# Holding back the first pair's two output stores in a single-core Winograd convolution

## The chip, the cores and the metric

The kernel runs on one core of a Trainium2 chip. The metric is the device time of one execution in microseconds (us), given as the median of several runs. A core has a matrix engine (TensorE, PE in the profile), three engines for elementwise work (VectorE or DVE, ScalarE or ACT, GpSimd or POOL), SyncE (SP), which here only issues transfers, and 16 DMA engines, which move everything between device memory and the on-chip memory.

## The reference

The kernel computes a 3x3 convolution with padding 1 over 16 images of 64 channels and 64x64 points, with 128 output channels, all float32:

```python
batch, c_in, h, w, c_out = 16, 64, 64, 64, 128
x_pad = np.pad(x, ((0, 0), (0, 0), (1, 1), (1, 1)), mode='constant')
...
output[b, co] += weight[co, ci, kh, kw] * x_pad[b, ci, kh:kh+h, kw:kw+w]
```

The input is 16.8 MB and the output 33.6 MB, so two thirds of the traffic are stores.

## The kernel before

**Pairs and blocks.** The images are taken two at a time: a pair's two images of 64 channels fill the 128 partitions. There are 8 pairs (`p`), and each is worked through in 4 blocks (`blk`) of 16 output rows. In a block, TensorE makes three groups of products per image, `U`, `A` and `Bt` (L154), each into a PSUM tile (tag `acc`; 8 such buffers). The row direction uses a short Winograd scheme: `U` comes from sums of neighbouring input rows (`ss`, made on GpSimd at L73 one pair ahead), and even and odd output rows are `A + U` and `Bt + U`. ScalarE copies `U` out of PSUM (`ut`, L168), and VectorE adds (L177 for even rows, L180 for odd rows) into the output tile `ot`.

**Output tiles.** Every image has its own `ot` tile of 128 x 4096 float32 (2 MB). They come in turn from `opool`, which has 7 buffers. The first two of these are lent to the float32 inputs of pairs 0 and 1 (`x0`, `x1`). So the buffers run: `x0`, `x1`, pair 0 (third and fourth), pair 1 (fifth and sixth), pair 2 (seventh and first), pair 3 (second and third), pair 4 (fourth and fifth), and so on. The first image of pair 0 and the second image of pair 3 share a buffer: the second L177 instruction of pair 3 may only write when the store of pair 0's first image has landed. Likewise pair 4's first image waits for the store of pair 0's second image.

**Transfers and their queues.** SP issues the loads of the weights and of `x0` and `x1` (L44 to L48). GpSimd issues the other six input loads (L59, pairs 2 to 7) one behind the other at the start; these read 2 MB of float32 each and write 1 MB of float16. The stores (L112) have two queues. For pairs 0 to 5 an image is stored whole, after its last block: the first image by SP (`store(nc.sync, ...)`, L182), the second by ScalarE. ScalarE's store is put into the list `held` (L184) and issued in the next block behind the two `ut` copies (L170, L171), so that ScalarE need not wait for VectorE. Pairs 6 and 7 are stored in halves of 1 MB. `keep` fixes the order of the instructions of an engine as it is written.

**Semaphores.** The transfers of SP and ScalarE take turns on a set of eight completion semaphores. A store that takes one up again first waits until the transfer that had it eight issues earlier has landed.

Of the kernel before, what the change touches and what calls it, by code (L numbers as in the profile page):

```python
# [12 lines left out]
@with_exitstack  # L13
def kernel(
    ctx: ExitStack,
    tc: tile.TileContext,
    x: bass.AP,
    weight: bass.AP,
    out: bass.AP,
):  # L20
    nc = tc.nc
    B, CI, H, W = x.shape
    CO = weight.shape[0]
    assert H == 64 and W == 64 and CI == 64 and CO == 128 and B % 2 == 0
    NP = B // 2
    RB = 8

    keep = tc.keep_in_program_order
    x_rows = x.rearrange("b c h w -> (b c) h w")
    out_rows = out.rearrange("b co h w -> b co h w")  # L30
    w_flat = weight.rearrange("co ci kh kw -> co (ci kh kw)")

    const = ctx.enter_context(tc.tile_pool(name="const", bufs=1))
    psum = ctx.enter_context(tc.tile_pool(name="psum", bufs=8, space=bass.MemoryType.PSUM))
    xpool = ctx.enter_context(tc.tile_pool(name="xpool", bufs=8))
    opool = ctx.enter_context(tc.tile_pool(name="opool", bufs=7))
    spool = ctx.enter_context(tc.tile_pool(name="spool", bufs=3))
    upool = ctx.enter_context(tc.tile_pool(name="upool", bufs=4))


    first = const.tile([48, 16], F32)
    nc.scalar.dma_start(first, x_rows[5 * 128 :: 8, 0, 0:16])
    w_raw = const.tile([CO, CI * 9], F32)
    nc.sync.dma_start(w_raw, w_flat)  # L44
    x0 = opool.tile([128, H, W], F32, tag="ot", name="x0")
    nc.sync.dma_start(x0, x_rows[0:128, :, :])
    x1 = opool.tile([128, H, W], F32, tag="ot", name="x1")
    nc.sync.dma_start(x1, x_rows[128:256, :, :])  # L48
    cuts = [(0, 18), (18, 34), (34, 50), (50, 64)]
    ident = const.tile([128, 128], F16)  # L50
    make_identity(nc, ident)
    w16 = const.tile([CO, CI * 9], F16)
    keep(nc.gpsimd.tensor_copy(w16, w_raw))  # L53

    xs = {0: xpool.tile([128, H, W], F16, tag="xs", name="xs")}

    def load(p):
        xs[p] = xpool.tile([128, H, W], F16, tag="xs", name="xs")
        keep(nc.gpsimd.dma_start(xs[p], x_rows[128 * p : 128 * p + 128, :, :]))  # L59

    xs[1] = xpool.tile([128, H, W], F16, tag="xs", name="xs")
    for p in range(2, NP):
        load(p)


    ss = {}

    def sums(eng, p, src, lo, n):
        if p not in ss:
            ss[p] = spool.tile([128, H // 2, W], F16, tag="ss", name="ss")  # L70
        v = src.rearrange("p (j i) c -> p j i c", i=2)
        keep(
            eng.tensor_add(  # L73
                ss[p][:, lo : lo + n, :], v[:, lo : lo + n, 0, :], v[:, lo : lo + n, 1, :]
            )
        )


    Wt = const.tile([128, 5, 3, CO], F16)
    G0, G21, G1, G01, G2 = range(5)  # L80

    def wrow(i):
        return Wt[:, i, :, :].rearrange("p t c -> p (t c)")

    wps = {}
    for kh in (1, 2, 0):
        wp = psum.tile([128, 512], F32, tag="acc", name="wp")
        for k in range(3):
            t = 3 * kh + k
            for q in (0, 64):  # L90
                nc.tensor.matmul(wp[q : q + 64, k * CO : k * CO + CO], w16[:, t::9], ident)  # L91
        wps[kh] = wp[:, 0 : 3 * CO]
    keep(nc.scalar.copy(wrow(G1), wps[1]))  # L93
    sums(nc.vector, 0, x0, 0, RB)
    keep(nc.vector.tensor_sub(wrow(G21), wps[2], wrow(G1)))  # L95
    keep(nc.vector.tensor_sub(wrow(G01), wps[0], wrow(G1)))  # L96
    for n, (lo, hi) in enumerate(cuts):
        keep(nc.scalar.copy(xs[0][:, lo:hi, :], x0[:, lo:hi, :]))  # L98
        if n == 0:
            keep(nc.scalar.copy(wrow(G0), wps[0]))  # L100
            keep(nc.scalar.copy(wrow(G2), wps[2]))  # L101
        if n < 3:
            sums(nc.vector, 0, x0, RB * (n + 1), RB)

    held = []

    whole = {3: (0, 64)}
    halves = {1: (0, 32), 3: (32, 64)}
    cuts_of = [(whole, whole)] * (NP - 2) + [(halves, halves)] * 2

    def store(eng, p, b2, ot, lo, hi):
        return eng.dma_start(  # L112
            out_rows[2 * p + b2, :, lo:hi, :],
            ot.rearrange("p j i c -> p (j i) c")[:, lo:hi, :],
        )

    for p in range(NP):
        if p + 1 < NP:
            for lo in (0, 16):
                sums(nc.gpsimd, p + 1, x1 if p == 0 else xs[p + 1], lo, 16)  # L120
        ots = [
            opool.tile([128, H // 2, 2, W], F32, tag="ot", name="ot") for _ in range(2)
        ]
        for blk in range(4):
            j0 = blk * RB

            def group(wi_rows):

                tiles = [
                    psum.tile([128, RB, W], F32, tag="acc", name="acc") for _ in range(2)  # L130
                ]
                n = 3 * len(wi_rows)
                i = 0
                for wi, off in wi_rows:
                    for kw in (1, 0, 2):
                        c_lo, c_hi = max(0, 1 - kw), min(W, W + 1 - kw)
                        for b2 in range(2):
                            p0 = 64 * b2
                            lo, hi = j0, j0 + RB
                            if off is None:  # L140
                                rhs = ss[p][p0 : p0 + 64, lo:hi, c_lo + kw - 1 : c_hi + kw - 1]
                            else:
                                while 2 * lo + off < 0:
                                    lo += 1
                                while 2 * (hi - 1) + off > H - 1:
                                    hi -= 1
                                first = 2 * lo + off
                                last = 2 * (hi - 1) + off
                                rhs = xs[p][
                                    p0 : p0 + 64,  # L150
                                    first : last + 1 : 2,
                                    c_lo + kw - 1 : c_hi + kw - 1,
                                ]
                            nc.tensor.matmul(  # L154
                                tiles[b2][:, lo - j0 : hi - j0, c_lo:c_hi],
                                Wt[p0 : p0 + 64, wi, kw, :],
                                rhs,
                                start=i == 0,
                                stop=i == n - 1,
                            )  # L160
                        i += 1
                return tiles

            U = group([(G1, None)])
            us = []
            for b2 in range(2):
                ut = upool.tile([128, RB, W], F32, tag="ut", name="ut")
                keep(nc.scalar.copy(ut, U[b2]))  # L168
                us.append(ut)
            while held:  # L170
                keep(store(nc.scalar, *held.pop(0)))  # L171
            if p == 0 and blk >= 2:
                for lo in (32 * blk - 64, 32 * blk - 48):
                    keep(nc.scalar.copy(xs[1][:, lo : lo + 16, :], x1[:, lo : lo + 16, :]))  # L174
            A = group([(G21, 1), (G0, -1)])
            for b2 in range(2):
                nc.vector.tensor_add(ots[b2][:, j0 : j0 + RB, 0, :], A[b2], us[b2])  # L177
            Bt = group([(G01, 0), (G2, 2)])
            for b2 in range(2):
                nc.vector.tensor_add(ots[b2][:, j0 : j0 + RB, 1, :], Bt[b2], us[b2])  # L180
            if blk in cuts_of[p][0]:
                store(nc.sync, p, 0, ots[0], *cuts_of[p][0][blk])  # L182
            if blk in cuts_of[p][1]:
                held.append((p, 1, ots[1], *cuts_of[p][1][blk]))  # L184
    while held:
        keep(store(nc.scalar, *held.pop(0)))
# [30 lines left out]
```

## Time and profile before

| what | value |
|---|---|
| time, median of 3 runs | 127.02 us (126.86 to 127.49) |
| profiled execution, its own time | 127.1 us |
| profiled execution, span of the instructions | 125.3 us |
| TensorE busy | 105.8 us (84%) |
| VectorE busy | 83.5 us (67%) |
| ScalarE busy | 44.5 us (36%) |
| GpSimd busy | 34.5 us (28%) |
| device memory read, written | 17.08 MB, 33.55 MB |
| a whole-image store, median from issue to landing | 20.3 us (SP), 20.1 us (ScalarE) |
| one input load of pairs 2 to 7, median from issue to landing | 29.7 us |

The profile was taken on one execution of 127.1 us, of which 125.3 us lie between its first and last instruction; the other 1.8 us lie outside. It is 0.1 us above the median of the runs. Times inside the profile count from the start of the span. DMA figures are given as the busy share of the 16 engines and as GB/s; the GB/s count the bytes written, so that a load which turns float32 into float16 shows half of what it reads.

### The profile page before, as it was taken

Reading aid. Unit: us, or ns where it says so; the run is one execution under the profiler, and the core shown is the slowest. Engines: PE = TensorE matmul, PEld = TensorE weight load, DVE = VectorE, ACT = ScalarE, POOL = GpSimd, SP = SyncE. Lnnn points to the kernel's source line nnn. Section 1 sums busy time; section 2 is a strip of 40 time slices with the busy share of each in tenths; the row PEclk is TensorE's granted clock in tenths of the full one; section 3 lists DMA queues with packets and bytes.
Section 4 is the critical chain, followed back from the end, with each engine's and each line's share of the span. In section 5 each row is a group of like instructions: output and inputs, shape, how many; then the busy total and the mean of one; then the engine's idle time right before and its main releaser. Section 6 shows DMA issues by size and latency. Waiting matters only on the chain.

```text
span 125.3 us, 2411 instructions
## 1 busy us (share of the span) xinstructions
PE 105.8 (84%) x978; PEld 53.8 (43%) x978; DVE 83.5 (67%) x134; ACT 44.5 (36%) x76; POOL 34.5 (28%) x27
## 2 busy tenths in 40 slices
PE   0407999999999999999999999999999999996000
PEld 0303454555455454555555455454545455452000
DVE  0009298787778777777787778788788878868000
ACT  4108938943333333333333333333333333331000
POOL 2750008999366005700480049000000000000000
PEclk9999999999999999999999999999999999999965
DMA  4999999999999999999999999999999999999980
GB/s 121 424 379 332 316 267 225 212 209 204 377 340 387 356 332 358 356 379 340 340 377 356 405 434 424 429 439 439 413 429 429 424 416 416 431 424 418 431 371 39
DMA packets 4250, 44.48 MB, mean 355 GB/s; under 512 B 528, under 2 KB 528, under 8 KB 656
## 3 DMA queue, kind: packets, MB, share of 16 engines
q1 hardware_dynamic: 1872, 21.27, 40.8%
q10 hardware_dynamic: 1504, 16.78, 31.6%
q0 software_dynamic: 864, 6.29, 24.6%
q8 instruction: 7, 0.11, 0.3%
q14 instruction: 3, 0.02, 0.0%
HBM read 17.08 MB, written 33.55 MB: 404 GB/s over the span
## 4 chain that ended last, share of the span: by engine, by line
PE 82%; DMA 7%; DVE 2%; issue 1%; DVEq 0%; SPq 0%
PE acc L154 82%; DMA x<-in_x_dram 7%; DVE ot L177 1%; DVE ss L73 1%; DVE ot L180 0%; DVEq L212 0%; SPq L44 0%; DVEq L177 0%
## 5 line engine op out<-in xcount | busy, mean ns | idle before, releaser
L154 PE MATMUL acc<-xs,Wt 64*128 64x504 f16 (+3 forms) x768 | 88.6, 377 | 0.0
L154 PEld LDWEIGHTS <-Wt 64*128 64x128 f16 x960 | 52.7, 95 | 55.8 <-issue 6.1
L177 DVE TENSOR_TENSOR ot<-acc,ut 128x512 f32<-128x512 f32 x64 | 41.2, 686 | 23.1 <-PE acc L154 18.4
L168 ACT COPY ut<-acc 128x512 f32<-128x512 f32 x64 | 34.4, 589 | 60.6 <-issue 38.5
L180 DVE TENSOR_TENSOR ot<-acc,ut 128x512 f32<-128x512 f32 x64 | 41.1, 684 | 0.0
L73 POOL TENSOR_TENSOR ss<-xs 128x1024 f16<-128x1024 f16 x12 | 25.2, 2122 | 28.9 <-PE acc L154 25.8
L154 PE MATMUL acc<-ss,Wt 64*128 64x504 f16 (+1 forms) x192 | 27.0, 384 | 4.3 <-DVE ss L73 4.3
L73 DVE TENSOR_TENSOR ss<-x 128x512 f16<-128x512 f32 x4 | 2.6, 685 | 9.5 <-DMA x<-in_x_dram 9.5
L73 POOL TENSOR_TENSOR ss<-x 128x1024 f16<-128x1024 f32 x2 | 4.7, 2358 | 11.5 <-DMA x<-in_x_dram 11.5
L98 ACT CAST xs<-x 128x1024 f16<-128x1024 f32 (+2 forms) x4 | 4.0, 1054 | 3.7 <-DMA x<-in_x_dram 3.7
L91 PE MATMUL wp<-ident,w 128*64 128x128 f16 x18 | 1.3, 327 | 4.6 <-POOL w L53 4.6
L174 ACT CAST xs<-x 128x1024 f16<-128x1024 f32 x4 | 4.0, 1058 | 0.0
L59 POOL DMA_DIRECT2D xs<-in_x_dram x6 | 3.4, 582 | 0.0
L91 PEld LDWEIGHTS <-w 128*64 128x64 f16 x18 | 1.1, 209 | 4.6 <-POOL w L53 4.6
L93 ACT ACT_TABLE_LOAD x1 | 1.3, 1283 | 1.2 <-PEq L201 1.2
L93 ACT CAST Wt<-wp 128x384 f16<-128x384 f32 x1 | 0.5, 479 | 2.8 <-PE wp L91 2.8
L53 POOL CAST w<-w_raw 128x576 f16<-128x576 f32 x1 | 0.7, 664 | 2.6 <-DMA w_raw<-in_weight_dram 2.6
L100 ACT CAST Wt<-wp 128x384 f16<-128x384 f32 x1 | 0.5, 478 | 0.5 <-DVE Wt L96 0.5
L95 DVE TENSOR_TENSOR Wt<-wp,Wt 128x384 f16<-128x384 f32 x1 | 0.6, 550 | 0.0
L96 DVE TENSOR_TENSOR Wt<-wp,Wt 128x384 f16<-128x384 f32 x1 | 0.5, 547 | 0.0
L101 ACT CAST Wt<-wp 128x384 f16<-128x384 f32 x1 | 0.5, 485 | 0.0
masks.py:199 POOL TENSOR_SCALAR_AFFINE_SELECT ident<-ident 128x128 f16<-128x128 f16 x1 | 0.3, 293 | 0.1
(5 smaller groups left out, 0.6 us busy)
## 6 DMA issues: line engine op xcount, KB each, us to landing
out_dram<-ot SPq DMA_DIRECT2D x6, 2048.0 KB, 20.3
out_dram<-ot ACTq DMA_DIRECT2D x6, 2048.0 KB, 20.1
xs<-in_x_dram POOLq DMA_DIRECT2D x6, 1024.0 KB, 29.7
x<-in_x_dram SPq DMA_DIRECT2D x2, 2048.0 KB, 13.0
out_dram<-ot SPq DMA_DIRECT2D x4, 1024.0 KB, 10.9
out_dram<-ot ACTq DMA_DIRECT2D x4, 1024.0 KB, 10.9
w_raw<-in_weight_dram SPq DMA_DIRECT2D x1, 288.0 KB, 3.1
first<-in_x_dram ACTq DMA_DIRECT2D x1, 3.0 KB, 2.9
```

The costliest lines, as they stand in the source:

```text
L53: keep(nc.gpsimd.tensor_copy(w16, w_raw))
L59: keep(nc.gpsimd.dma_start(xs[p], x_rows[128 * p : 128 * p + 128, :, :]))
L73: eng.tensor_add(ss[p][:, lo : lo + n, :], v[:, lo : lo + n, 0, :], v[:, lo : lo + n, 1, :])
L91: nc.tensor.matmul(wp[q : q + 64, k * CO : k * CO + CO], w16[:, t::9], ident)
L93: keep(nc.scalar.copy(wrow(G1), wps[1]))
L95: keep(nc.vector.tensor_sub(wrow(G21), wps[2], wrow(G1)))
L98: keep(nc.scalar.copy(xs[0][:, lo:hi, :], x0[:, lo:hi, :]))
L154: nc.tensor.matmul(tiles[b2][:, lo - j0 : hi - j0, c_lo:c_hi], Wt[p0 : p0 + 64, wi, kw, :], rhs, start=i == 0, stop=i == n - 1,)
L168: keep(nc.scalar.copy(ut, U[b2]))
L174: keep(nc.scalar.copy(xs[1][:, lo : lo + 16, :], x1[:, lo : lo + 16, :]))
L177: nc.vector.tensor_add(ots[b2][:, j0 : j0 + RB, 0, :], A[b2], us[b2])
L180: nc.vector.tensor_add(ots[b2][:, j0 : j0 + RB, 1, :], Bt[b2], us[b2])
```

## The change

The two stores of pair 0 are issued later, and both by ScalarE. Before, SP issued the store of pair 0's first image as soon as VectorE had finished it, and ScalarE issued the second image's store in the first block of pair 1. Now both are put into `held`, and `held` is not emptied until block 3 of pair 1, where ScalarE issues both behind its two `ut` copies. From there on everything is issued in the places where it was, so that pair 1's stores follow a block later.

```diff
-            while held:
+            while held and (p, blk) >= (1, 3):
                 keep(store(nc.scalar, *held.pop(0)))
...
-            if blk in cuts_of[p][0]:
+            if p == 0 and blk == 3:
+                held.append((p, 0, ots[0], 0, 64))
+            elif blk in cuts_of[p][0]:
                 store(nc.sync, p, 0, ots[0], *cuts_of[p][0][blk])
```

## The prediction

> **What bounds the kernel now.** I read first the page's slices of the span and its DMA queues, then the chain of work that ended last, then the busy time of chosen stretches, then landing times of single transfers, and last the timelines of VectorE and TensorE around the place where the moved store's buffer is needed again.
>
> The page's slices (40 of 3.13 us each; busy tenths, then GB/s written) and queues (packets, MB, share of the 16 engines):
>
> ```profile
> DMA  4999999999999999999999999999999999999980
> GB/s 121 424 379 332 316 267 225 212 209 204 377 340 387 356 332 358 356 379 340 340 377 356 405 434 424 429 439 439 413 429 429 424 416 416 431 424 418 431 371 39
> ...
> q1 hardware_dynamic: 1872, 21.27, 40.8%
> q10 hardware_dynamic: 1504, 16.78, 31.6%
> q0 software_dynamic: 864, 6.29, 24.6%
> ```
>
> The DMA engines are full from the second slice to the 38th; the three queues (SP, ScalarE, GpSimd) add up to 97% of 16 engines' span. The chain of waits, however, is nearly all TensorE:
>
> ```profile
> 10.21 103.29 PE acc L154 x948
> ```
>
> TensorE runs without a break from 10.2 to 113.5 us. Two limits therefore lie side by side, and the chosen stretches (length, then engines' busy time, clock, DMA share, GB/s written) show how close:
>
> ```profile
> 18.50:25.50 7.00, 7.00 (x68) 3.54 (x66) 5.71 (x10) 5.87 (x8) 6.15 (x3) 1.00 1.04 218
> 27.50:30.00 2.50, 2.50 (x28) 1.22 (x24) 2.01 (x4) 1.07 (x2) 2.50 (x2) 1.00 1.06 157
> 31.00:71.00 40.00, 40.00 (x379) 20.30 (x376) 31.66 (x51) 13.31 (x25) 13.97 (x7) 1.00 1.01 359
> 72.00:116.00 44.00, 42.68 (x402) 21.48 (x396) 34.95 (x56) 13.96 (x26) 4.20 (x2) 1.00 1.01 426
> 116.00:121.00 5.00, 0.00 (x0) 0.00 (x0) 0.04 (x1) 0.00 (x0) 0.00 (x0) 0.88 1.00 423
> 121.00:124.50 3.50, 0.00 (x0) 0.00 (x0) 0.00 (x0) 0.00 (x0) 0.00 (x0) 0.50 0.32 133
> ```
>
> Loads alone (18.5 to 25.5) write 218 GB/s, which is 436 read. Stores alone (72 to 116) move 426. Loads beside stores (31 to 71) write 359; GpSimd's last three loads fall there, and about 2.9 MB of what is written is theirs, so 73 GB/s more are read: 432. A byte costs the same in all three mixtures.
>
> The last stores are issued at 115.5 and 116.1 us and land at 124.2 and 124.4 us. From 116 on, 5.0 x 423 + 3.5 x 133 = 2.58 MB are still written; 2.10 MB of it are the two last stores themselves. Older backlog is thus only 0.48 MB, or 1.1 us. So the end moves with the DMA total, or with TensorE once TensorE is over 1.1 us later.
>
> **Part 1: the stores' bytes.** Nothing is added or removed: 20 stores before and after, the same sizes. Time is lost only if the DMA engines run empty, so I ask what they have to do between 25.8 us, where the stores were issued, and their new place. GpSimd's loads landed at 18.7, 24.1, 29.0, 42.5, 57.3 and 71.8 us (issue plus landing time of each). Without stores beside them, two follow each other by 4.9 us (24.1 to 29.0); with both store queues full, by 13.5 to 14.8 us. Without the stores, the last three would land at 33.9, 38.8 and 43.7 us. ScalarE issues the held stores behind the copies of pair 1's block 3: those start at 35.40, and at 25.75 the same pair of copies had its store 0.68 us later, so at 36.1, and the second 0.34 us later (one issue lasts 338 to 367 ns). The loads last till 43.7, so the engines stay full. Cost: 0. Loads that come earlier than before help nobody, since TensorE never waits for one after 10.2 us.
>
> **Part 2: the issuing engines.** SP loses one issue (0.33 us) that nothing waited for. Its store of pair 1's first image keeps its own place at 38.6. ScalarE loses one issue at 26.4 and has two at 36.1, 0.7 us in all. Behind them on ScalarE are the copies at 38.56, before which it sat idle for 2.09 us, so 1.4 us of cover remain. Without it, the 0.34 us more would be late into a PSUM buffer. Cost: 0. The semaphores go round in the same order as before, and the uses that come eight issues later wait for pair 0's stores at 77 us, long after any landing considered here.
>
> **Part 3: the wait for the buffer.** This is what the change can lose. Pair 3's second image takes the buffer of pair 0's first. Its need, on VectorE:
>
> ```profile
> 52.71 1.29 DVE L177 TENSOR_TENSOR ot<-acc,ut 128x512 f32<-128x512 f32 x2 [0.69 <-PE acc L154]
> ```
>
> The second of these two adds starts at 53.3 us. Before, the store had landed at 25.8 + 20.5 = 46.3, which left 7.0 us. Now it is issued 10.3 us later.
>
> ```profile
> L112 SPq DMA_DIRECT2D out_dram<-ot x1: 348/348/348, 25.8 to 25.8; - x1
> ...
> DMA to landing us min/median/max: 20.5/20.5/20.5
> ```
>
> With the same 20.5 us it would land at 56.6. With the longest landing of any whole-image store (22.9 us, issued at 51.4) it would land at 59.0; with the shortest (13.9 us, issued at 89.9, with two queues full) at 50.0. Between these I work it out. A 2 MB store costs the engines 2.10 / 426 = 4.9 us. The page's slices show that stores did not get going before about 30.1 us (204 GB/s up to 31 is still the loads' own rate), 4.3 us behind the issue. So the first held store starts at 40.4, when 43.7 - 40.4 = 3.3 us of loads remain. SP's store of pair 1 starts at 38.6 + 4.3 = 42.9. Until then two queues share: 1.25 us of work each. Then three share: the loads' 2.05 us take until 49.1, and the store has 1.6 us left, which at half the engines end at 52.3. The first store of the trace landed 1.5 us after the same reckoning (30.1 + 3 x 4.9 = 44.8 against 46.3), so I add 1.5: it lands at 53.8, half a microsecond late. I take this rather than a row of before, since before three loads stood against the store, and now two thirds of one.
>
> What does half a microsecond cost? TensorE's timeline:
>
> ```profile
> 51.12 2.69 PE L154 MATMUL acc<-xs,Wt 64*128 64x512 f16 x24
> ...
> 54.28 2.77 PE L154 MATMUL acc<-xs,Wt 64*128 64x512 f16 x24
> ```
>
> (The shapes that each row names are those of its first matmul.) A block takes six of the eight PSUM buffers. What the late add frees is next taken by the following block's `Bt`, the second half of the stretch that starts at 54.28, so at 55.6. The add ends at 54.0 in time, so it may be 1.6 us late before TensorE stops: landings up to 54.9 cost nothing there, and VectorE, idle about 0.7 us in each block, catches up. With the 1.1 us at the end, the end itself stays where it is for landings up to 56.0. Cost at 53.8: 0.
>
> Pair 0's second store follows on ScalarE's queue at half the engines: 52.3 + 9.8 + 1.5 = 63.6, needed at 65.4. Pair 1's second image, third on that queue, by the same steps at 73, needed at 78.2. Cost: 0.
>
> **Sum.** 127.1 + 0 + 0 + 0 = 127.1 us on the profiled execution, which stands 0.1 above the median; I forecast 127.1.
>
> **Rivals.** *Late landing, slower.* If the engines serve ScalarE's queue worse than by equal shares, the landing takes its length of before or more. At 56.6, TensorE is 1.7 us late and the end 0.6 us (127.7); at 59.0, 4.1 and 3.0 (130.1). It decides from a landing at 56.0. For it: 10 of the 12 whole-image stores took 16 us or more. Against it: those stood behind more work. The Trainium skill, "DMA: Bandwidth & Descriptors", section "Rules for kernel authors", speaks against the change here: it advises to issue a DMA early and to wait for its semaphore late. No run yet shows that rule in this kernel; by it one would forecast this rival.
>
> *Restarts, slower.* The stretch 27.5 to 30.0, just when the first stores came in, wrote 157 GB/s against 218: 28% of 2.5 us, 0.7 us lost. Before, the store queues never ran empty after that. Now SP's queue is one store lighter and starts alone at 38.6, and by the shares above is empty near 64 and again near 77 and 90. One more such loss gives 127.8, four 129.9. Against it: from 102.7 to 116.1 the queues are nearly empty and are refilled, and still move 423 to 426.
>
> *A gain.* That 0.7 us may not come back when the stores begin against two thirds of a load instead of three. The limit is the backlog: with none, the last stores end 1.1 us earlier, at 126.0. I give 126.4 for the 0.7. For it: the dip stands exactly there. Against it: stores still start beside a load.
>
> *The change does nothing that it says*: the engines' instruction lists show both stores behind pair 1's block 3 on ScalarE, and nothing else moved; I give this no chance.
>
> **How the numbers follow.** Forecast 0.60; late landing 0.14, restarts 0.13, gain 0.13. About 0.5% (0.6 us) is what a measurement of this kernel can tell from no change. The late landing at 56.6 just passes that bound, and so do all other rivals, so the classes are: faster 0.13, same 0.60, slower 0.27. For 8 in 10, the range takes in the gain of 0.7 with some of its limit (126.2), and of the slower cases all but the far halves, to a landing of 57.7 us or two and a half restarts: 128.8.
>
> **What would show each step.** Right: loads at 33.9, 38.8 and between 46 and 50 us; GB/s near 215 till 40; the first held store landing near 54; TensorE's chain still ending near 113.5 and the last store at 124.4. Late landing: VectorE's L177 waits for a transfer at 53.3 for over 1.6 us, and TensorE's chain ends later. Restarts: slices below 400 GB/s after 60 us. Gain: no slice near 157 at 38 to 42 us, and the last landing before 123.8. If the DMA engines show idle time between 26 and 116 us, Part 1 is wrong.

## The result, and the profile after

| | before | after |
|---|---|---|
| time, median of 6 runs each (least to most) | 127.19 us (126.86 to 127.49) | 127.82 us (127.75 to 128.07) |
| profiled execution (span) | 127.10 us (125.3) | 127.75 us (125.9) |

The ratio after to before is 1.0055, 95% interval 1.0037 to 1.0073: slower by 0.7 us. That is inside the predicted range, and about the 0.5% that was taken as no change (the interval holds values on both sides of it). The forecast's sum was off by one term of 0.7 us, and none of the rivals holds its cause.

First what the prediction watched. The page's slices of the kernel after (3.15 us each; DMA busy tenths, GB/s written), its queues (packets, MB, share of 16 engines), and its chain:

```profile
DMA  5999999999999999999999999999999999999970
GB/s 143 399 377 328 338 255 211 221 211 216 224 208 203 341 377 421 422 435 416 432 427 427 427 442 422 432 432 416 432 422 432 422 409 419 424 419 403 409 323 13
...
q1 hardware_dynamic: 1728, 19.17, 36.5%
q10 hardware_dynamic: 1648, 18.88, 35.4%
q0 software_dynamic: 864, 6.29, 24.3%
...
10.36 103.70 PE acc L154 x948
```

The loads now run alone up to 41 us (203 to 224 GB/s written) and are done after 51; from there on nearly everything that moves is stores. The engines stay full. TensorE's chain starts 0.15 us later and ends at 114.06 instead of 113.50. That looks like the answer and is not, as experiment 2 shows.

The chosen stretches (length, busy time of PE, PEld, VectorE, ScalarE and GpSimd, clock, DMA share, GB/s written):

```profile
36.00:43.00 7.00, 7.00 (x70) 3.66 (x68) 5.56 (x9) 2.81 (x6) 4.20 (x2) 1.00 1.04 248
48.00:71.00 23.00, 23.00 (x220) 11.88 (x216) 18.25 (x30) 7.51 (x14) 8.41 (x4) 1.00 1.01 427
72.00:116.00 44.00, 43.25 (x406) 22.12 (x402) 34.50 (x56) 14.17 (x27) 4.21 (x2) 1.00 1.01 425
116.00:121.00 5.00, 0.00 (x0) 0.00 (x0) 0.61 (x2) 0.00 (x0) 0.00 (x0) 0.64 0.96 401
121.00:124.50 3.50, 0.00 (x0) 0.00 (x0) 0.00 (x0) 0.00 (x0) 0.00 (x0) 0.50 0.32 136
```

Between 72 and 116 the rate is that of before (425 against 426), and 121 to 124.5 looks the same too (136 against 133). The stretch 116 to 121 is the first that differs: 401 GB/s at a share of 0.96, against 423 at 1.00. Some engines have nothing left for a moment although stores are outstanding. Finer stretches of the tail show who is late; first of before, then of after:

```profile
122.00:123.00 1.00, 0.00 (x0) 0.00 (x0) 0.00 (x0) 0.00 (x0) 0.00 (x0) 0.50 0.33 139
123.00:124.00 1.00, 0.00 (x0) 0.00 (x0) 0.00 (x0) 0.00 (x0) 0.00 (x0) 0.50 0.06 25
124.00:125.00 1.00, 0.00 (x0) 0.00 (x0) 0.00 (x0) 0.00 (x0) 0.00 (x0) 0.50 0.00 0
```

```profile
122.00:123.00 1.00, 0.00 (x0) 0.00 (x0) 0.00 (x0) 0.00 (x0) 0.00 (x0) 0.50 0.18 74
123.00:124.00 1.00, 0.00 (x0) 0.00 (x0) 0.00 (x0) 0.00 (x0) 0.00 (x0) 0.50 0.08 33
124.00:125.00 1.00, 0.00 (x0) 0.00 (x0) 0.00 (x0) 0.00 (x0) 0.00 (x0) 0.50 0.02 8
```

One engine at work is 1/16 of the share, 0.06, and about 427 / 16 = 27 GB/s. After, from 122 to 123 less is left than before (0.18 against 0.33), so most engines are done earlier; yet a single engine goes on until 124.6. The whole loss is that engine's tail.

**The packets.** The trace also records single DMA packets. A store packet of 16 KB nearly always takes 611 or 624 ns while loads run beside it. While no load is under way, a second kind appears: packets of 628 to 700 ns, 648 on average. They follow one another without overlap (but for a short stretch in some traces: 97.2 to 98.5 us in after), and about 8 of them fit into 5 us (5 / 0.648 = 7.7): that is the whole output of one of the 16 engines, 6% slower than the others. Some ten packets of a trace (16 in early_act) take over 700 ns; the counts of slow packets and their excess leave them out. Slow packets in stretches of 5 us from 40 to 100 us (by their start), with the loads' data packets beside them (by their end):

```
              40 45 50 55 60 65 70 75 80 85 90 95
before  slow   0  1  0  0  0  1  8  8  8  7  8  8
        loads 37 51 40 42 48 39  1  0  0  0  0  0
after   slow   0  3  8  8  8  7  8  8  8  7  8 10
        loads 61 21  0  0  0  0  0  0  0  0  0  0
```

Each transfer leaves 16 packets of 4 bytes behind its data in the records (24 transfers of SP and ScalarE, 384 such packets), which reads as one for each engine. If the bytes are dealt evenly too, the slow engine falls behind for as long as it is slow. Before, the last load landed at 71.8 us; after, at 7.24 + 43.7 = 50.9. These 21 us are 32 packets of 648 ns, at 37 ns more than 611 each: 1.2 us. Counted in the records, the slow engine's excess is 2.00 us before (54 packets) and 3.29 after (89).

The 54 and 89 are the 16 KB packets alone. When the half stores follow, with packets of 8 KB, the row goes on: in before, from 103.7 to 115.0 us, a nearly unbroken row of packets takes about 320 to 340 ns each, where the others take 309. There it ends, 0.3 us behind TensorE's last matmul (114.7). In three other traces (before_stretch3, before_stretch5 and after_quarter7_b, experiments 6, 7 and 9) it also ends 0.2 to 0.5 us behind it, and in after_short (experiment 2), where the last matmul ends at 110.6, the row ends at 110.9. So "no load under way" may be only half of the condition, and a working TensorE the other half; no run tests that by itself. It also means that the engine which ends last isn't slow any more at the end: its packets of the last 4 us take 309 ns, before and after. It is late by what it lost earlier. The records name no engine, so that the late one is the slow one is inferred, from the sums at the end of the experiments.

### The profile page after: what moved, and what is told of

It reads as the page before. It is cut to its first block, busy times and chain, and to the rows that moved or that the text cites. A ratio compares the mean times of both kernels' runs of the same rounds, so it can differ in the third digit from the quotient of the medians.

```text
span 125.9 us, 2411 instructions
## 1 busy us (share of the span) xinstructions
PE 106.2 (84%) x978; PEld 54.7 (43%) x978; DVE 83.7 (66%) x134; ACT 44.5 (35%) x76; POOL 34.5 (27%) x27
## 4 chain that ended last, share of the span: by engine, by line
PE 82%; DMA 7%; DVE 2%; issue 1%; DVEq 0%; SPq 0%
PE acc L154 82%; DMA x<-in_x_dram 7%; DVE ot L177 1%; DVE ss L73 1%; DVE ot L180 0%; DVEq L214 0%; SPq L44 0%; DVEq L177 0%
## 5 line engine op out<-in xcount | busy, mean ns | idle before, releaser
L154 PEld LDWEIGHTS <-Wt 64*128 64x128 f16 x960 | 53.6, 96 | 55.5 <-issue 6.6
```

What stands on the lines that cost most here:

```text
L154: nc.tensor.matmul(tiles[b2][:, lo - j0 : hi - j0, c_lo:c_hi], Wt[p0 : p0 + 64, wi, kw, :], rhs, start=i == 0, stop=i == n - 1,)
```

## The experiments

Theories, as the expectations name them. **A**: the end follows TensorE, whose chain ran 0.56 us later, since `x0` landed later and the full clock was granted at 14.99 us instead of 13.99. **B**: one DMA engine ends late because of the change; **B1** because ScalarE's queue now carries more of the load, **B2** because the stores are late at all. **C**, formed from the packets of the first runs: the slow engine is slow only once no load is under way, and late stores let the loads end early. All ratios are to the kernel before, on the same chip, with their 95% interval.

**1. The changed kernel once more** (`after_again`, no edit).

> The changed kernel once more. In its profile TensorE got its full clock at 15.0 us (before: 14.0) and ran 0.56 us later from there to the end, and one DMA engine worked alone for the last 1.6 us. Theory A (clock): the end follows TensorE, so an execution in which the full clock comes at about 14 us takes 127.2 us. Theory B (one late DMA engine): 127.8 us whenever the clock comes, and again a single engine that lands the last half store over 1 us behind the others.

127.98 against 127.14 us, 1.0065 (1.0047 to 1.0083). The full clock came at 14.68 us this time, 0.3 earlier than in the first profile, and the time is no lower: against A. 89 slow packets again, the last packet's end at 124.90.

**2. The changed kernel with less work for TensorE at the end** (`after_short`). The last pair's third column tap is left out.

```diff
-                n = 3 * len(wi_rows)
+                taps = (1, 0) if p == NP - 1 else (1, 0, 2)
+                n = len(taps) * len(wi_rows)
...
-                    for kw in (1, 0, 2):
+                    for kw in taps:
```

> The changed kernel with the products of the third column tap (kw = 2) of the last pair left out, all stores kept: TensorE has 40 matmuls less, VectorE's 2.5 us for a block become the pace, and the last stores are issued some 2.8 us earlier. Theory A (the end follows TensorE): 125.0 to 125.5 us. Theory B (the end is one DMA engine's total work): at least 127.2 us, that engine's last packets land at the same time as before.

127.65 us, 1.0050 (1.0031 to 1.0070). The last matmuls in TensorE's timeline (start, length), first of after and then of this run, ScalarE's last store in its timeline, and the tail:

```profile
112.56 2.69 PE L154 MATMUL acc<-xs,Wt 64*128 64x512 f16 x24
```

```profile
108.74 1.85 PE L155 MATMUL acc<-xs,Wt 64*128 64x512 f16 x16
```

```profile
113.07 0.34 ACTq L112 DMA_DIRECT2D out_dram<-ot  x1
```

```profile
121.00:122.00 1.00, 0.00 (x0) 0.00 (x0) 0.00 (x0) 0.00 (x0) 0.00 (x0) 0.50 0.63 262
122.00:123.00 1.00, 0.00 (x0) 0.00 (x0) 0.00 (x0) 0.00 (x0) 0.00 (x0) 0.50 0.18 74
123.00:124.00 1.00, 0.00 (x0) 0.00 (x0) 0.00 (x0) 0.00 (x0) 0.00 (x0) 0.50 0.06 25
```

TensorE's last matmul ends at 110.6 us, 4.7 us sooner than in the kernel after (115.3; the chain of waits leaves TensorE earlier, at 114.06), and the last store is issued 3.6 us sooner (113.07 against 116.64). The end hardly moves: again 0.18, then one engine alone, till 125.05. A is refuted; the end is one DMA engine's.

**3. The queues evened out** (`late_balanced`). In the changed kernel, SP takes over the store of pair 1's second image.

```diff
-            if blk in cuts_of[p][1]:
+            if p == 1 and blk == 3:
+                store(nc.sync, p, 1, ots[1], 0, 64)
+            elif blk in cuts_of[p][1]:
                 held.append((p, 1, ots[1], *cuts_of[p][1][blk]))
```

> Pair 0's two stores late on ScalarE as in the changed kernel, but pair 1's second image is issued by SP, so that each queue again has ten stores. Theory B1 (the load of the two queues: SP's runs empty and starts again): the loss is gone, 127.2 us. Theory B2 (the lateness itself: engines that had only loads for 10 us): 127.8 us as in the changed kernel. Theory A (clock) expects no difference but by the moment of the clock.

127.82 us, 1.0067 (1.0048 to 1.0087): no better. B1 falls.

**4. Both stores on ScalarE, but early** (`early_act`). The changed kernel without the hold: ScalarE issues both in block 0 of pair 1.

```diff
-            while held and (p, blk) >= (1, 3):
+            while held:
```

> Only the other half of the change: pair 0's first image is issued by ScalarE too, but both in block 0 of pair 1 as early as before (26.4 and 26.8 us). Theory B1 (load of the queues): 127.8 us. Theory B2 (lateness): 127.2 us. Theory A: no difference but by the moment of the clock.

127.23 us, 1.0008 (0.9996 to 1.0020). So the queue costs nothing that can be measured and the lateness does: B2. The trace also speaks against A once more: the full clock came at 15.91 us and TensorE's chain ended at 114.40, both later than in after, in an execution of 127.19 us. The loads ended at 64.9 us and there were 67 slow packets, between before (71.8, 54) and after (50.9, 89). By theory C alone the 13 packets more would give 0.47 us; 0.1 was measured, and where the rest went is open.

**5. The loads drawn out** (`before_stretch`). The test of C with the opposite sign: nothing is done to the stores, but the loads of pairs 5 and 6 are cut into halves. Their packets are then half as big, and the loads should last longer beside full store queues; they did.

```diff
-        keep(nc.gpsimd.dma_start(xs[p], x_rows[128 * p : 128 * p + 128, :, :]))
+        cut = H // {5: 2, 6: 2}.get(p, 1)
+        for r in range(0, H, cut):
+            keep(
+                nc.gpsimd.dma_start(
+                    xs[p][:, r : r + cut, :], x_rows[128 * p : 128 * p + 128, r : r + cut, :]
+                )
+            )
```

> The kernel before, with the loads of pairs 5 and 6 cut in two (rows 0 to 31, 32 to 63), so that GpSimd's queue has packets of half the size and moves more slowly beside the stores. Loads should land until some 90 us instead of 71.5; the stores are issued where they were. Theory C (from the traces' packet records: one of the 16 DMA engines takes about 648 ns instead of 611 ns for a store packet of 16 KB, but only once the last load is through; it is the engine that ends last): some 20 us less of that, 0.9 us less on that engine, and the time falls by 0.5 to 0.9 us below the kernel before, to 126.3 to 126.7 us. Theory B2 (the lateness of the first stores as such, the DMA engines' mix before 40 us): 127.1 us, no change.

126.56 against 127.03 us, 0.9964 (0.9952 to 0.9977): faster than both kernels. Its slices and its tail:

```profile
GB/s 143 394 381 329 318 281 213 213 208 218 389 406 380 358 387 398 398 348 387 398 373 366 396 356 344 358 345 413 415 426 437 437 402 415 423 429 423 434 418 118
```

```profile
122.00:123.00 1.00, 0.00 (x0) 0.00 (x0) 0.00 (x0) 0.00 (x0) 0.00 (x0) 0.50 0.51 213
123.00:123.50 0.50, 0.00 (x0) 0.00 (x0) 0.00 (x0) 0.00 (x0) 0.00 (x0) 0.50 0.05 16
123.50:124.00 0.50, 0.00 (x0) 0.00 (x0) 0.00 (x0) 0.00 (x0) 0.00 (x0) 0.50 0.00 0
```

Slices under 400 GB/s written, which show a load under way, reach to 84 us now (the last load lands at 89.3). There are 31 slow packets instead of 54, and the engines end nearly together: half the share still from 122 to 123, and nothing after 123.5.

**6 and 7. More and less of the same.** `before_stretch5` cuts pair 5's load alone (`{5: 2}`), `before_stretch3` those of pairs 5, 6 and 7 (`{5: 2, 6: 2, 7: 2}`).

> As the run with the loads of pairs 5 and 6 cut in two, but only that of pair 5: the last load should land at about 81 us, half the shift. Theory C: half the gain, 126.6 to 126.9 us. Theory B2: 127.1 us.

> The kernel before with the loads of pairs 5, 6 and 7 cut in two: the last load should land at about 97 us instead of 88 (pairs 5 and 6 cut) or 71.5. Theory C: the slow engine has another 10 us less, but with pairs 5 and 6 cut it already ended with the others (last landings 122.3 to 123.4 us), so the gain is used up: 126.3 to 126.6 us, within 0.2 us of that run. If instead the time keeps falling by another 0.4 us, one slow engine is not the whole of it.

Pair 5 alone: 127.04 us, 0.9991 (0.9976 to 1.0007). The traced execution, at 126.72 with 39 slow packets, fits; the median doesn't, so this size stays inconclusive. All three: 126.62 us, 0.9966 (0.9953 to 0.9979), with 16 slow packets. As C has it, there is nothing more to gain once the slow engine isn't last; the mean packet time per engine meanwhile rises from 122.51 to 122.75 us.

**8. Smaller store packets** (`small_stores`). In the kernel before, the whole-image stores of pairs 0 to 2 go as two transfers of 32 rows, so that here the loads get the larger share.

```diff
     def store(eng, p, b2, ot, lo, hi):
+        if p < 3 and hi - lo == 64:
+            keep(store(eng, p, b2, ot, 0, 32))
+            lo = 32
```

> The kernel before, its stores issued where they were, but the whole-image stores of pairs 0 to 2 cut in two, each half a DMA of its own. Their packets are half as big, so the loads beside them get a half of the engines instead of a third and should end at about 58 us instead of 71.5. Theory C: 13 us more with the slow engine, 127.5 to 127.8 us, although no store is late. Theory B2: 127.1 us.

127.75 us, 1.0054 (1.0040 to 1.0068): the loads ended at 62.4 us, and the time is where C puts it. It proves less than it seems to, for the smaller packets have a price of their own: beside loads, two of 8 KB take 309 or 322 ns each where one of 16 KB takes 611 or 624, and the mean per engine is 0.27 us more. For it speaks that the row of slow packets starts at 62 us, just when the loads end: 32 of 314 to 349 ns among the 8 KB packets up to 77 us, 0.62 us of excess, and 1.82 us in 16 KB packets (49).

**9. The changed kernel mended** (`after_quarter7`, `after_quarter7_b` and `after_quarter7_c`, one kernel). The late stores stay, and pair 7's load is cut into quarters to make it last (the edit of experiment 5 with `{7: 4}`).

> The changed kernel, its late stores kept, with the load of pair 7 cut into four, so that what is left of it when the stores begin (3 us of the engines' work) has packets of a quarter of the size and lasts until some 65 to 70 us instead of 50.6. Theory C: the time returns to within 0.2 us of the kernel before (127.0 to 127.3 us), since the loads end at the same time as there. Theory B2 (lateness as such): 127.8 us as in the changed kernel.

> Once more the changed kernel with the load of pair 7 in four, for a second trace: its first execution took 127.21 us with store packets over 628 ns from 72 us on, the other six 127.7 to 128.1 us. Theory C: an execution of 127.7 us or more has its last load packets near 50 us, or its slow packets from some 50 us on; one of 127.2 us has them from about 70 us on. If an execution of 127.8 us has slow packets only from 70 us on, theory C does not account for the change's loss.

> The same kernel a third time, for a third trace; same expectation as for the second.

127.86 us, 1.0065 (1.0050 to 1.0080), where C had expected 127.0 to 127.3: a miss. The other two traced executions took 127.78 each, with the row of slow packets only from 67 to 69 us on, which the expectation had named as what C doesn't account for. The packets offer an account, found only afterwards. The excess fell as C says, from 3.29 to 1.8 to 2.1 us, but the 512 packets of 2 KB that the cut makes took 200 to 206 ns on average (median 172), where a quarter of the 625 ns of an 8 KB load packet would be 156, and the mean per engine rose from 121.72 to between 122.70 and 123.14. In place of one late engine, 9 of the 16 were still at work at 123.0 us in the second trace, and 6 at 123.5. So C is left standing on the excess, its forecast of the time fell, and this mend is no mend. It is not shown that the whole loss of the change goes away when its loads last longer.

**10. One load moved, nothing else** (`load7_late`). In the kernel before, pair 7's load is issued after pair 6's sums, so that a gap without loads opens in the middle of the stores and closes again.

```diff
-    for p in range(2, NP):
+    for p in range(2, NP - 1):
         load(p)
...
+        if p == 5:
+            load(7)
```

> The kernel before with its stores as they were and all loads whole, but GpSimd issues the load of pair 7 only after the sums of pair 6 (about 65 us), so that from 57 us (load of pair 6 landed) to 66 us no load is under way, and from 66 to about 80 us one is again. Theory C: the one engine's slow store packets (628 to 700 ns) appear from about 57 to 66 us, are gone while the last load runs, and come back at about 80 us; the stretch without loads is as long in all as before, so the time stays at 127.0 us within 0.3. If the slow packets do not go away with the load, or do not appear in the gap, the loads are not what hides them.

127.20 against 127.08 us, 1.0011 (0.9996 to 1.0025): the load-free time is about as long as before, and so is the run. The gap, and the stretch with load 7 under way (issued at 65.7, landed 20.4 us later):

```profile
57.50:65.00 7.50, 7.50 (x73) 3.74 (x71) 6.04 (x11) 2.56 (x5) 3.49 (x2) 1.00 0.99 419
71.00:84.00 13.00, 13.00 (x126) 6.49 (x123) 10.23 (x17) 4.49 (x9) 0.00 (x0) 1.00 1.01 355
```

The packets in stretches of 5 us:

```
              40 45 50 55 60 65 70 75 80 85 90 95
slow           0  1  0  7  8  8  1  0  0  7  8  8
loads         40 56 32  2  0  0 44 40 44  0  0  0
```

Off, on, off with the load, on again, within one execution: it is the load under way that makes the engine keep up, not the place in the program, the queue or the age of the run. (TensorE works throughout these stretches: its part is not tested here.)

All of it side by side (profiled executions, us). "Excess" is what the slow packets took over 611 ns each; "mean" is the packet time per engine, averaged over 16:

| kernel | last load landed | slow packets | excess | mean | last packet ends | time |
|---|---|---|---|---|---|---|
| before_stretch3 | 97 | 16 | 0.63 | 122.75 | 123.59 | 126.62 |
| before_stretch | 89.3 | 31 | 1.09 | 122.51 | 123.40 | 126.40 |
| before_stretch5 | 80.8 | 39 | 1.44 | 122.29 | 123.58 | 126.72 |
| load7_late | 86.1 (gap 58 to 66) | 53 | 1.95 | 122.22 | 124.05 | 127.21 |
| before | 71.8 | 54 | 2.00 | 121.99 | 123.96 | 127.10 |
| early_act | 64.9 | 67 | 2.47 | 121.97 | 124.06 | 127.19 |
| after | 50.9 | 89 | 3.29 | 121.72 | 124.60 | 127.75 |
| after_again | 52.4 | 89 | 3.24 | 121.77 | 124.90 | 128.03 |
| late_balanced | 51.6 | 87 | 3.21 | 121.97 | 124.92 | 128.24 |
| after_short | 51.4 | 89 | 3.33 | 121.73 | 125.05 | 128.18 |

Mean plus excess gives the last packet's end within 0.5 us in every row (before 123.99 against 123.96, after 125.01 against 124.60). It is a rough sum, and it has the order right but for neighbours that lie within 0.4 us. Experiments 8 and 9 are not in the table: there it gives 124.70 against 124.58 (small_stores, with the 0.62 us of its 8 KB packets), and 124.52, 125.27 and 124.99 against 124.07, 124.65 and 124.64 (after_quarter7 and its repeats), up to 0.62 us too late, about as much as the whole loss.

## Why the prediction was right and wrong

**Part 1 failed, and only there.** "A byte costs the same in all three mixtures" is true of the mean of 16 engines (425 to 436 GB/s) and not of each engine. With stores alone, while TensorE works, one of them is 6% slower, and the end waits for one that is late. The cost of the moved bytes was put at 0 and measured about +0.7 us: 1.29 us more excess, less 0.27 us by which the mean fell, less what the rough sum misses. The question asked there, whether the engines run empty, was answered correctly: they were full till 116 us. It was the wrong question, since full engines can still finish at different times. The mixture had been read at 72 to 116 us, where the slow engine was already at work, and an average of 426 could not show it. That 127.82 lies in the range is luck as far as this goes: the room up to 128.8 was left for a late landing and for restarts, and neither happened.

**The end.** "The end moves with the DMA total, or with TensorE once TensorE is over 1.1 us later": neither moved it. The bytes were the same, the packet time per engine fell by 0.27 us, and experiment 2 shows that the end stays even when TensorE ends 4.7 us earlier. The last store landed at 125.0 instead of 124.4. (The 113.5 us at which TensorE was said to end is where the chain leaves it; its last matmul ended at 114.7.) The 0.48 MB of backlog, 1.1 us, was an average as well; the slow engine's own backlog was larger.

**Part 2 held.** Both stores were issued at 36.08 and 36.48 us (predicted 36.1 and 0.34 later), and experiments 3 and 4 show that neither the queue nor its balance costs anything that can be measured.

**Part 3 held, closely.** The first held store:

```profile
L112 ACTq DMA_DIRECT2D out_dram<-ot x1: 367/367/367, 36.1 to 36.1; - x1
...
DMA to landing us min/median/max: 17.8/17.8/17.8
```

It landed at 53.9 us (predicted 53.8), and the adds that need its buffer:

```profile
53.27 1.42 DVE L177 TENSOR_TENSOR ot<-acc,ut 128x512 f32<-128x512 f32 x2 [0.69 <-PE acc L154]
```

1.42 us for the two instead of 1.29: a wait of 0.13 us, and none on TensorE (busy for 23.00 of the 23.00 us from 48 to 71). That it is 0.13 and not the predicted 0.5 is luck: TensorE ran 0.56 us later in this execution, and with it the need. The second held store landed at 63.0 (63.6), pair 1's second image at 69.8 (73). Of the loads, 34.0 and 39.1 us were as predicted, and the last, at 50.9, was a little past the end of its "between 46 and 50". That number was worked out in order to place the stores, and its other meaning, that the stores would run alone for 21 us longer, went unread.

**The rivals.** *Late landing* did not happen. The Trainium skill's advice there ("DMA: Bandwidth & Descriptors", "Rules for kernel authors", to issue a DMA early and wait for it late) was right in sign, since the early issue is faster, but not through its wait, which cost 0.13 us on an engine with idle time. *Restarts* did not happen: no slice lies under 400 GB/s between 60 us and the tail. *A gain* happened in part: at the stores' first packets, ten microseconds later than before, the rate dipped less.

```profile
37.50:40.00 2.50, 2.50 (x28) 1.36 (x26) 2.27 (x4) 0.88 (x2) 2.50 (x2) 1.00 1.11 200
```

That is 200 GB/s, where before's row of 27.5 to 30.0 had 157. But the engines were busy in both (shares of 1.11 and 1.06), so that the 0.7 us which the prediction took for lost was not idle time. The mean fell by 0.27 us, and the slow engine took more than that back.

## What to carry to other kernels

- When the DMA engines bound a kernel, as here, its end is the end of the latest of the 16, and a mean over them hides it. Read the tail in stretches of half a microsecond: a share stuck near 0.06 is one engine working alone.
- In such a kernel, moving a transfer also moves what it shared the engines with: ask which mixture gets longer and which shorter, and whether every engine does equally well in each. Here it paid a little to keep loads running beside the stores (before_stretch, 0.9964).
- A chain of waits that is 82% TensorE, and a TensorE that is late by just the time lost, do not show that TensorE sets the end; shortening TensorE's work showed that here it does not.

## What the runs showed of the hardware

- One of the 16 DMA engines took about 648 ns for a 16 KB store packet where the others took 611, but only while no load of GpSimd's queue was under way; beside a load all were alike (experiment 10). Its 8 KB packets took about 320 to 340 ns against 309, and only until TensorE stopped (115.0 us in before, 110.9 in after_short). The records don't name the engine, and why it is slow stays open. The Trainium skill ("DMA: Bandwidth & Descriptors", "Latency and other measured facts") has two engines usually slower, and ties it, as its best guess, to transfers of GpSimd's kind. Here it is one, and it is slow only when none of those is under way.
- Loads with smaller packets fell behind beside full store queues, and their bytes cost more: halving two loads' packets moved the last landing from 71.8 to 89.3 us, and 2 KB packets took 200 to 206 ns on average where a quarter of an 8 KB packet's time would be 156.
- The moment at which the full clock was granted differed from run to run (13.99 us before, 14.99 and 14.68 after, 15.91 in early_act), and the end of TensorE's chain with it (113.50, 114.06, 113.86 and 114.40), without moving the time of this kernel.
